# Low halves of column weights in two instructions, and the first attention unit's order tied to the last column, in a hybrid decoder step

## The chip, the core and the metric

The kernel runs on one core of a Trainium2 chip. Its engines are TensorE (PE, matrix products; PEld is its loading of weights), VectorE (DVE), ScalarE (ACT), GpSimd (POOL) and SyncE (SP, which here only issues DMAs). Each engine works through its own instructions in the order in which they were written out, and waits on semaphores for what the others make. The metric is the time of one execution on the device, in microseconds (us).

## The reference: what is computed

One step of a decoder layer for a prompt of 1024 rows of width 1024 and for 8 samples that each add one row. One input projection feeds three groups of heads; their outputs are gated, put side by side and projected back.

```python
h    = rms_norm(x, ln_g)
proj = h @ w_in                                   # 1024 x 3480
q, kv, gates, z_nsa, u, z_rw, q_mem, z_mem = split_in(proj)
# 8 heads: compressed blocks, selected blocks (top 16 of 64 rows), window of 512
o_nsa = gate_mix(sigmoid(gates), o_compressed, o_selected, o_window)
# 4 heads: S <- S diag(w) + (S(-kk)) (kk*a)^T + v k^T ;  y = S r, row after row
o_rw  = rwkv7_mix(u, ...)
# 4 heads: cross attention into 256 memory tokens
o_mem = softmax(q_mem @ k_mem.T) @ v_mem
cat   = concat(o_nsa * silu(z_nsa), o_rw * silu(z_rw), o_mem * silu(z_mem))
y     = x + cat @ w_out
```

With a prompt of 1024 rows there are 16 blocks of 64, so in the prompt all blocks that causality allows are selected. New key and value rows, the recurrent state and the memory's keys and values are outputs too.

## The kernel before

**Phase 1 projects.** `w_in` is taken in columns of 128. For each, `w_load` (L275) loads 512 KB into a raw buffer `wraw` (two buffers) from SP's queue, and `w_split` makes two float32r parts of it: ScalarE copies the high half `whi` (L283), VectorE subtracts to get the low half `wlo` (L284, 128 x 1024 in one instruction; one of the first columns gives it to GpSimd). `project` then goes through eight slices of the depth, k = 0 to 7, for each half of the prompt (512 rows): three matmuls a slice into `p_pr` (`h_k` high by `whi`, `h_k` low by `whi`, `h_k` high by `wlo`). PSUM holds three such buffers. A column of the gates z is finished by `do_z`: tanh on ScalarE (L318), one operation on VectorE (L319), stores to `z_d` (L321, L323). Row norms run on VectorE in many small instructions (L126 to L137), keys and queries are rotated at L384 to L400.

**What it is woven with.** The recurrent group works in four quarters (`rwkv_prep`, `rwkv_state`), with products `p_it`, `p_iy` on TensorE and copies `iT`, `iY`, `Ti` on the other engines between them (L920 to L967). `drive` takes its steps at a higher priority (AHEAD = 400), and the columns' steps fill in between. The keys, the compressed blocks and the memory's keys and values follow, with the last columns between them.

**The first unit.** An attention unit is a tile of 128 rows, a group of keys and a pair of heads, (i, g, hp); the units run from i = 7 down. For each head h of the pair and branch b (0 selected, 1 window), `attn_scores` makes scores `p_s` (keys split in `kh` and `kl`; two PSUM buffers of 1024), masks them and takes the row maximum on VectorE (L1502, called a mask from here on), then the exponential on ScalarE (L1508), a reciprocal (L1533), and a scaling on GpSimd (L1540). The transposes `p_pT` and their copies `pt` (VectorE L1464, ScalarE L1462) follow, then the products `p_o`. `first_scores` runs the scores of unit (7, 0, 0) between the steps of the last column, at the steps AT = (1, 5, 8, 11). The compressed branch goes through `p_sc` and `pcq` (L1419 to L1439).

**What sets the order.** Matmuls run in the order in which they are written (`InOrder` ties each to the one before it); on the other engines a scheduler chooses by priority, data and buffers, and `high_priority` moves what is inside it ahead. `in_turn` ties a step to the previous one of a chain kept in `self.mask`. In phase 2 the transposes have three PSUM banks (`pT`) and `p_o` has one (`pO`); the order of units is written out, with side work in four lanes (`step`, `slot`). Memory attention takes its maxima at L1596 on VectorE and its exponentials at L1598 on ScalarE.

## Time and profile before

| | us |
|---|---|
| median of 3 runs | 923.46 |
| runs | 923.26, 928.93, 923.46 |
| the profiled execution, whole | 927.17 |
| its span in the trace | 925.4 |
| TensorE busy in it | 888.4 |
| VectorE busy in it | 646.1 |
| ScalarE busy in it | 440.1 |

The trace is that of one execution, whose time lies above the median. A row of the timeline gives the start in us from the span's start, the duration, the engine, the line, the operation with output and inputs, and in brackets the engine's idle time before it with what ended that. The table of windows gives for each stretch its length and the busy time of TensorE, its weight loads, VectorE, ScalarE and GpSimd, then the granted TensorE clock, the DMA share and the GB/s. Where short instructions follow each other, a duration overlaps the next start a little; the difference of the starts is what an engine spends.

### The profile page before, as it was taken

What the parts mean: (1) busy time and instruction counts of PE and PEld (TensorE: products, weight loads), DVE (VectorE), ACT (ScalarE), POOL (GpSimd) and SP (SyncE); (2) the same over time, 40 slices, a digit from 0 to 9 for tenths busy, and PEclk for the clock granted to TensorE, in tenths of its full rate; (3) what the DMA queues carried; (4) which work ended last, traced back from release to release, by engine and by line L of the source; (5) the groups of instructions that cost most, each with busy time, mean ns of one, the idle gap of its engine ahead of it and who ended that gap; (6) DMA issues with size and microseconds to landing.
All of it is one profiled execution on the core that took longest, in us unless ns stands there. A gap on an engine that the chain in (4) does not pass through costs nothing.

```text
span 925.4 us, 24648 instructions
## 1 busy us (share of the span) xinstructions
PE 888.4 (96%) x9839; PEld 757.6 (82%) x9839; DVE 646.1 (70%) x2002; ACT 440.1 (48%) x1006; POOL 188.9 (20%) x280
## 2 busy tenths in 40 slices
PE   8999999999999999989998999999999998999998
PEld 8998888877878788758986788888878887887976
DVE  7768778964776459957567877676778986548454
ACT  7654324232443233324436676667666775324311
POOL 2000000000000000000105454444455665112010
PEclk9999999999999999999999999999999999999999
DMA  7431304141321303635638314422120037887561
GB/s 280 127 84 35 101 29 126 47 127 49 81 91 39 91 14 114 144 95 151 166 95 247 120 37 140 134 83 78 54 66 16 25 93 222 292 258 211 174 241 49
DMA packets 128298, 107.01 MB, mean 116 GB/s; under 512 B 26385, under 2 KB 113112, under 8 KB 128056
## 3 DMA queue, kind: packets, MB, share of 16 engines
q1 hardware_dynamic: 123096, 93.43, 34.7%
q0 software_dynamic: 3296, 10.75, 3.3%
q8 instruction: 78, 1.28, 0.6%
q10 hardware_dynamic: 1792, 1.26, 0.5%
q14 instruction: 36, 0.29, 0.1%
HBM read 84.72 MB, written 22.78 MB: 116 GB/s over the span
## 4 chain that ended last, share of the span: by engine, by line
PE 71%; DVE 17%; ACT 6%; issue 3%; DMA 1%; POOL 1%; SPq 0%; DVEq 0%; ACTq 0%; POOLq 0%
PE p_pr L87 26%; PE p_out L87 9%; PE p_s L87 5%; PE p_o L87 4%; PE p_pT L87 4%; PE p_hid L87 4%; ACT p L1508 3%; DVE p L1502 3%; PE p_pr L307 2%; PE p_tk L87 1%; DMA wraw<-in_w_in_dram 1%; DVE pt L1464 1%; PE p_it L87 1%; PE p_iy L87 1%; PE p_z L87 1%
## 5 line engine op out<-in xcount | busy, mean ns | idle before, releaser
L87 PE MATMUL p_pr<-h,whi 128*128 128x512 f32 (+2 forms) x1168 | 280.7, 334 | 2.0 <-DVE zt L319 2.0
L87 PEld LDWEIGHTS p_pr<-h,whi 128*128 128x128 f32 x1168 | 189.9, 189 | 21.0 <-issue 2.6
L87 PE MATMUL p_pr<-h,wlo 128*128 128x512 f32 (+2 forms) x584 | 188.1, 325 | 0.6 <-DVE wlo L284 0.6
L87 PEld LDWEIGHTS p_pr<-h,wlo 128*128 128x128 f32 x584 | 109.8, 189 | 10.4 <-DVE wlo L284 0.8
L1540 POOL TENSOR_SCALAR p<-p,fac,gates 128x640 f32<-128x640 f32 (+7 forms) x124 | 100.1, 819 | 77.4 <-DVE fac L1533 57.5
L1508 ACT ACTIVATE p<-p,nm 128x640 f32<-128x640 f32 (+7 forms) x124 | 89.2, 720 | 41.8 <-DVE nm L1502 38.0
L87 PE MATMUL p_pT<-ident,p 128*128 128x128 f32 x528 | 72.2, 279 | 8.4 <-DVE pt L1464 3.1
L1122 POOL MEMSET w2d<- 128x128 f32 x1 | 0.2, 208 | 375.7 <-DVE rq_r L137 375.7
L87 PEld LDWEIGHTS p_pT<-ident,p 128*128 128x128 f32 x528 | 56.6, 140 | 20.8 <-issue 6.0
L87 PE MATMUL p_o<-pt,vs 128*64 128x128 f32 x1056 | 68.4, 278 | 0.4 <-DVE cat L1578 0.4
L1502 DVE CUSTOM_DVE_ANT_0 p<-p_s,bmask 128x512 f32<-128x512 f32 (+7 forms) x96 | 60.6, 660 | 6.7 <-PE p_s L87 6.1
L87 PE MATMUL p_s<-kh,qs 128*128 128x512 f32 (+3 forms) x191 | 64.4, 350 | 0.8 <-DVE nm L1502 0.8
L283 ACT ACTIVATE whi<-wraw 128x1024 fp32r<-128x1024 f32 x34 | 36.0, 1059 | 60.0 <-PE p_pr L87 47.8
L87 PEld LDWEIGHTS p_o<-pt,vs 128*64 128x64 f32 x1056 | 57.3, 137 | 7.7 <-issue 3.8
L284 DVE TENSOR_TENSOR wlo<-wraw,whi 128x1024 fp32r<-128x1024 f32 x33 | 40.3, 1222 | 30.9 <-ACT whi L283 30.9
L87 PE MATMUL p_s<-kl,qs 128*128 128x512 f32 (+3 forms) x192 | 60.2, 334 | 0.0
L1464 DVE COPY pt<-p_pT 128x512 f32<-128x512 f32 (+1 forms) x72 | 48.1, 671 | 11.3 <-PE p_pT L87 11.1
L87 PE MATMUL p_out<-woh,chi 128*128 128x512 f32 x128 | 51.7, 404 | 0.0
L87 PE MATMUL p_out<-woh,clo 128*128 128x512 f32 x128 | 50.2, 392 | 0.4 <-DVE clo L2446 0.4
L87 PE MATMUL p_out<-wol,chi 128*128 128x512 f32 x128 | 49.9, 390 | 0.0
L1462 ACT ACTIVATE pt<-p_pT 128x512 f32<-128x512 f32 (+1 forms) x72 | 41.0, 576 | 13.5 <-PE p_pT L87 12.8
L87 PEld LDWEIGHTS p_s<-kh,qs 128*128 128x128 f32 x191 | 36.1, 189 | 3.5 <-DVE nm L1502 1.0
(554 smaller groups left out, 1789.7 us busy)
## 6 DMA issues: line engine op xcount, KB each, us to landing
wraw<-in_w_in_dram SPq DMA_DIRECT2D x34, 512.0 KB
pg<-in_c_pool_dram SPq DMA_DIRECT2D x32, 256.0 KB
pg<-in_c_pool_dram SPq DMA_DIRECT2D x48, 128.0 KB
x<-in_x_prompt_dram SPq DMA_DIRECT2D x8, 512.0 KB
z_d<-zt SPq DMA_DIRECT2D x16, 256.0 KB
cat<-z_d SPq DMA_DIRECT2D x8, 512.0 KB
xres<-in_x_prompt_dram POOLq DMA_DIRECT2D x16, 256.0 KB, 3.5
out_dram<-xres POOLq DMA_DIRECT2D x16, 256.0 KB, 3.4
```

What stands on the lines that cost most here:

```text
L87: self.last = getattr(self.engine, op)(*a, **k)
L283: nc.scalar.activation(hi[:, :, :n], raw[:, :, :n], AF.Copy)
L284: (low or nc.vector).tensor_tensor(lo[:, :, :n], raw[:, :, :n], hi[:, :, :n].bitcast(F32), op=OP.subtract)
L307: self.last_mm = self.pe.matmul(ps[:m, :b - a], w[:, k, :m], h[k][:, a:b], start=(k == 0 and i == 0), stop=(k == 7 and i == 2))
L1122: nc.gpsimd.memset(w2d[:], 0.0)
L1462: nc.scalar.activation(pt[:, :n], ps[:, :n], AF.Copy)
L1464: nc.vector.tensor_copy(pt[:, :n], ps[:, :n])
L1502: return V.tensor_tensor_reduce(halves(x), halves(ps), m, -1.0, 3.0e38, op0=OP.add, op1=OP.min, accum_out=nm[:, h, b:b + 1])
L1508: e = self.e_last = A.activation(x, x, AF.Exp, scale=-1.0, bias=nm[:, h, b:b + 1], accum_out=sm[:, h, b:b + 1])
L1540: self.g_last = nc.gpsimd.tensor_scalar(x, x, f[:, h, b:b + 1], gate[:, hd + h, 1 + b:2 + b], op0=OP.mult, op1=OP.mult)
```

## The change

It has five parts.

1. `w_split` makes the low half in two instructions, of the slices k 0 to 3 and 4 to 7, where VectorE makes it. The one on GpSimd stays whole.
2. `do_z`'s operation on VectorE is ordered behind the chain of `in_turn`, once there is one, and the last of them becomes the chain's end when the last column is done.
3. The chain of masks and reciprocals now holds for both units with (i, g) = (7, 0), (7, 0, 0) too. `first_scores` takes its steps at priority FIRST, and reciprocal and scaling are held back (`held`) and released by the second mask of the next branch.
4. In phase 2, the matmuls are tied to the last one of phase 1, the pool `pO` is made ahead of `pT`, so that the banks are dealt out otherwise, and the side work's steps around unit 1's scores stand in another order.
5. `attn_mem` takes its maxima at priority FIRST.

```diff
@@ w_split
-        (low or nc.vector).tensor_tensor(lo[:, :, :n], raw[:, :, :n], hi[:, :, :n].bitcast(F32), op=OP.subtract)
+        for k in ((slice(0, 8),) if low else (slice(0, 4), slice(4, 8))):
+            (low or nc.vector).tensor_tensor(lo[:, k, :n], raw[:, k, :n], hi[:, k, :n].bitcast(F32), op=OP.subtract)
@@ do_z
-            nc.vector.scalar_tensor_tensor(t[:, a:b], t[:, a:b], 1.0, ps[:, :b - a], op0=OP.add, op1=OP.mult)
+            with self.tc.issue_after(self.mask.ins) if self.mask else ExitStack():
+                self.last_zv = nc.vector.scalar_tensor_tensor(t[:, a:b], t[:, a:b], 1.0, ps[:, :b - a], op0=OP.add, op1=OP.mult)
@@ phase1
-        self.last_kd = None
+        self.last_kd = self.mask = None
@@ first_scores
-        self.held, self.mask = [], None
+        self.held = []
...
             if n in AT:
-                next(gen, None)
+                with self.tc.high_priority(offset=FIRST):
+                    next(gen, None)
+                    if n == AT[-1]:
+                        self.held.pop()()
...
-        self.lasts = [x.ins for x in (self.r_last, self.e_last, self.g_last)]
+        self.lasts = [x.ins for x in (self.mask, self.e_last, self.g_last)]
+        self.mask = self.last_zv
@@ attn_scores
-        begin = (i, g, hp) == (7, 0, 1)
+        begin = (i, g) == (7, 0)
...
-            while self.held and h == 0:
+            while self.held and (b, h) == (1, 0):
                 self.held.pop()()
...
-                if begin:
-                    self.in_turn(recip)
-                else:
-                    self.r_last = recip()
+                self.in_turn(recip) if begin else recip()
...
-            if begin and b == 0:
+            if begin and (hp, b) != (1, 1):
                 self.held.append(scale)
@@ attn_mem
-            V.tensor_reduce(nm[:], ps[:], axis=AX.X, op=OP.max, negate=True)
+            with self.tc.high_priority(offset=FIRST):
+                V.tensor_reduce(nm[:], ps[:], axis=AX.X, op=OP.max, negate=True)
@@ phase2
+            self.pO = P("pO", 1, space=PSUM, side="right")
             self.pT = P("pT", 3, space=PSUM, side="right")
-            self.pO = P("pO", 1, space=PSUM, side="right")
...
-            self.te = InOrder(tc, nc.tensor, None)
+            self.te = InOrder(tc, nc.tensor, last)
...
-            for k in range(2):
-                next(start)
-                step(0)
+            next(start)
+            step(0)
+            next(start)
...
             for _ in start:
                 pass
+            step(0)
```

In the rows that follow, each is one instruction (or `x n` of a kind) in the order in which its engine takes them; lines of the kernel after stand up to six higher than the same lines before.

TensorE at the last column, before, from the last passes of slice 3 on. `p_s` are scores, those of unit 0 with 128 and 512 columns (the last of its window branch), those of unit 1 with 512 and 512:

```order
L87 MATMUL p_pr<-h_3_813,wlo 128x512
L87 MATMUL p_s<-kh_6225,qs 128x128
L84 MATMUL p_s<-kh_6225,qs 128x512
L87 MATMUL p_s<-kl_6226,qs 128x512
L87 MATMUL p_s<-kh_6228,qs 128x512
L87 MATMUL p_s<-kl_6229,qs 128x512
L87 MATMUL p_s<-kl_6226,qs 128x128
L87 MATMUL p_s<-kh_6228,qs 128x512
L87 MATMUL p_s<-kl_6229,qs 128x512
L87 MATMUL p_pr<-h_4_897,whi 128x512
```

Four passes of unit 1 have slipped between the first pass of unit 0 and its other three.

The same place of TensorE after, where slice 3 ends:

```order
L87 MATMUL p_pr<-h_3_818,wlo 128x512
L87 MATMUL p_s<-kh_6254,qs 128x128
L87 MATMUL p_s<-kl_6255,qs 128x128
L87 MATMUL p_s<-kh_6257,qs 128x512
L87 MATMUL p_s<-kl_6258,qs 128x512
L87 MATMUL p_pr<-h_4_903,whi 128x512
```

Unit 0's four passes stand together, and unit 1's come after the column's last slice:

```order
L87 MATMUL p_pr<-h_7_919,whi 128x512
L87 MATMUL p_pr<-h_7_920,whi 128x512
L87 MATMUL p_pr<-h_7_919,wlo 128x512
L87 MATMUL p_s<-kh_6254,qs 128x512
L87 MATMUL p_s<-kl_6255,qs 128x512
L87 MATMUL p_s<-kh_6257,qs 128x512
L87 MATMUL p_s<-kl_6258,qs 128x512
L87 MATMUL p_sc<-cmask 128x4x64
```

So the four passes of unit 1 have moved behind four slices of the projection.

VectorE at the last column, before. `ISA` of 1024 or 640 is a mask, `ISA` of 1 reads its maximum, `RECIPROCAL` is of unit 0, `zt` is `do_z`'s operation:

```order
L1502 ISA p_6999,p_7001<-p_s,bmask 128x1024
L1502 ISA p_7001 128x1
L319 SCALAR_TENSOR_TENSOR zt<-zt,p_pr 128x256
L1502 ISA p_7000,p_7001<-p_s,bmask 128x1024
L1502 ISA p_7001 128x1
L1533 RECIPROCAL p_7001<-p_7001 128x2
L319 SCALAR_TENSOR_TENSOR zt<-zt,p_pr 128x264
L1502 ISA p_7001<-p_s,bmask 128x640
L1502 ISA p_7001 128x1
L1502 ISA p_7002,p_7001<-p_s,bmask 128x640
L1502 ISA p_7001 128x1
L1533 RECIPROCAL p_7001<-p_7001 128x2
```

A `zt` stands between the first two masks, and the reciprocal of the selected branch is ahead of the window branch's masks.

VectorE there after:

```order
L1508 ISA p_7032,p_7034<-p_s,bmask 128x1024
L1508 ISA p_7034 128x1
L1508 ISA p_7033,p_7034<-p_s,bmask 128x1024
L1508 ISA p_7034 128x1
L321 SCALAR_TENSOR_TENSOR zt<-zt,p_pr 128x256
L321 SCALAR_TENSOR_TENSOR zt<-zt,p_pr 128x264
L1508 ISA p_7034<-p_s,bmask 128x640
L1508 ISA p_7034 128x1
L1539 RECIPROCAL p_7034<-p_7034 128x2
L1508 ISA p_7035,p_7034<-p_s,bmask 128x640
L1508 ISA p_7034 128x1
L1539 RECIPROCAL p_7034<-p_7034 128x2
```

The two masks of the selected branch stand together, both small `zt` behind them, and the reciprocal one mask later.

VectorE in the recurrent group's work, at 391 us of the trace, before. `nr_y` and `rq_a` are of a row norm, `iT` of the recurrent state:

```order
L127 TENSOR_SCALAR rq_g<-rq_a 128x1
L284 TENSOR_TENSOR wlo<-wraw,whi 128x1024
L384 TENSOR_TENSOR nr_y<-p_tk,rq_r 128x512
L128 TENSOR_SCALAR rq_a<-rq_a 128x1
L385 TENSOR_TENSOR nr_y<-nr_y,gains 128x512
L948 STREAM_TRANSPOSE iT<-p_it 128x256
```

The low half is one instruction ahead of the norm.

There, after:

```order
L127 TENSOR_SCALAR rq_g<-rq_a 128x1
L285 TENSOR_TENSOR wlo<-wraw,whi 128x512
L386 TENSOR_TENSOR nr_y<-p_tk,rq_r 128x512
L128 TENSOR_SCALAR rq_a<-rq_a 128x1
L285 TENSOR_TENSOR wlo<-wraw,whi 128x512
L387 TENSOR_TENSOR nr_y<-nr_y,gains 128x512
L954 STREAM_TRANSPOSE iT<-p_it 128x256
```

Its second part has moved behind two instructions of the norm. In the same way, the second part stands behind `iY`, `Ti` and `zt` at 318 us (where the whole one stood ahead of them), and behind three `zt` at 266 us.

More of the change, by code (lines that the diff above doesn't have):

```diff
@@ L1693, in phase2 @@
             self.load_z(7)
+            last = self.te.last
             self.te = nc.tensor
             self.attn_setup(P)
-            self.te = InOrder(tc, nc.tensor, None)
+            self.te = InOrder(tc, nc.tensor, last)
             units = [(i, g, hp) for i in range(7, -1, -1) for g in range(2) for hp in range(2)]
```

## The prediction

> **What bounds the kernel now.** I read the page first, then the windows of the stages that the change touches, then TensorE's waits, and the timeline at the longest of them.
>
> ```profile
> span 925.4 us, 24648 instructions
> PE 888.4 (96%) x9839; PEld 757.6 (82%) x9839; DVE 646.1 (70%) x2002; ACT 440.1 (48%) x1006; POOL 188.9 (20%) x280
> ...
> 240.00:280.00 40.00, 37.97 (x220) 32.36 (x219) 28.95 (x98) 15.70 (x28) 0.00 (x0) 0.96 0.30 88
> 480.00:520.00 40.00, 35.10 (x272) 29.13 (x271) 30.58 (x80) 22.09 (x49) 17.32 (x20) 1.00 0.79 232
> ```
>
> TensorE works 888.4 of 925.4 us, so all that a reordering can win is what lies in 37.0 us of gaps. The change leaves the number of matmuls as it is, and VectorE has 279.3 us idle (925.4 − 646.1): extra work there costs only where TensorE waits for it. The stage 480 to 520, where the first attention unit starts beside the last column, has 4.9 us of the gaps (40 − 35.10); the others that the change touches are single waits, shown below.
>
> **Part 1, the first unit.** Its rows on TensorE, each with the wait before it in brackets:
>
> ```profile
> 488.64 0.50 PE L84 MATMUL p_s<-kh,qs 128*128 128x512 f32 x1 [1.13 <-DVE p L1502]
> 495.75 0.38 PE L87 MATMUL p_sc<-cmask 128*128 128x256 f32 x1 [1.11 <-DVE zt L319]
> 497.46 0.66 PE L87 MATMUL p_pT<-ident,p 128*128 128x128 f32 x4 [0.47 <-DVE pcq L1422]
> 498.93 0.66 PE L87 MATMUL p_pT<-ident,p 128*128 128x128 f32 x4 [0.82 <-DVE pcq L1422]
> 500.36 0.66 PE L87 MATMUL p_pT<-ident,p 128*128 128x128 f32 x4 [0.77 <-ACT pt L1462]
> 509.77 0.66 PE L87 MATMUL p_pT<-ident,p 128*128 128x128 f32 x4 [0.60 <-DVE pt L1464]
> ```
>
> They sum to 4.90 us, which is the stage's whole gap. The first arises because unit 1's scores stand among the last four passes of unit 0's and wait for a score buffer that a mask holds. With the new order these four passes run together, the four slices `h_4` to `h_7` follow, and unit 1's scores come after them: the 1.13 us go. VectorE shows what then decides:
>
> ```profile
> 481.46 1.21 DVE L1502 CUSTOM_DVE_ANT_0 p<-p_s,bmask 128x1024 f32<-128x1024 f32 x1
> ...
> 484.26 0.42 DVE L319 SCALAR_TENSOR_TENSOR zt<-zt,p_pr 128x256 f32<-128x256 f32 x1 [1.58 <-ACT zt L318]
> 484.60 1.22 DVE L1502 CUSTOM_DVE_ANT_0 p<-p_s,bmask 128x1024 f32<-128x1024 f32 x1
> ...
> 490.46 0.82 DVE L1502 CUSTOM_DVE_ANT_1 p<-p_s,bmask 128x640 f32<-128x640 f32 x1 [1.88 <-PE p_s L87]
> ...
> 495.03 0.67 DVE L319 SCALAR_TENSOR_TENSOR zt<-zt,p_pr 128x512 f32<-128x512 f32 x1
> ```
> ```profile
> 492.76 0.40 PE L87 MATMUL p_pr<-h,wlo 128*128 128x512 f32 x1
> ...
> 505.74 1.97 PE L87 MATMUL p_o<-pt,vs 128*64 128x128 f32 x32
> ```
> ```profile
> 493.20 0.60 ACT L318 ACTIVATE zt<-p_pr 128x512 f32<-128x512 f32 x1 [0.66 <-PE p_pr L87]
> ...
> 495.13 1.15 ACT L1508 ACTIVATE p<-p,nm 128x1024 f32<-128x1024 f32 x1 [0.72 <-DVE nm L1502]
> ```
>
> Before, unit 0's second mask sits behind a `zt` that waits 1.58 us for ScalarE; with both masks in turn it starts at 482.7, when the first ends, instead of 484.60. The last mask of unit 0 waits for its scores: these come 1.13 plus about 1.0 us sooner (the stall, and unit 1's four score passes ahead of it at some 0.25 each, an estimate from the 0.50 of the first one shown, of which half overlaps). So it starts near 488.3 instead of 490.46 and ends at 489.1. The last `p_pr` ends near 491.0 (492.76 + 0.40 − 2.1). The large `zt` follows after its tanh (0.60) and its own 0.67, near 492.2 against 495.7, so `p_sc` no longer waits 1.11 for it.
>
> From there the chain is not TensorE's any more: a mask of 1.21, an exponential of 1.15, and both engines' copies between the transposes, while VectorE leaves few gaps. Laid out with these durations in the new order, the third group of transposes starts at 494.25 behind the `pcq` add (new wait 0.3), the fourth at 496.1 behind ScalarE, whose copy follows unit 1's first exponential (1.4), and the seventh at 501.4 behind a `pt` copy (1.65): 3.35 of new waits in place of 4.90, and `p_o` near 504.7 instead of 505.74. **−1.5 us.** Bounds: −4.9 if no new wait arises, and 0 if VectorE's chain, 30.58 of 40 us busy over the stage, only shifts the waits. I take the laid-out value, nearer to 0.
>
> The `pcq` multiply of the compressed branch goes behind the two masks of unit 2, 2.4 us:
>
> ```profile
> 505.18 1.58 DVE L1439 TENSOR_TENSOR pcq<-pcq,c_r 128x512 f32<-128x512 f32 x1
> ```
> ```profile
> 512.61 0.60 PE L87 MATMUL p_pT<-ident,pcq 128*128 128x128 f32 x4
> ```
>
> Its reader on TensorE starts 5.9 us after it ends, so I cost that at nothing; without that cover it would be 2.4 us, two masks. The swap of the two PSUM pools moves only addresses; the first `p_o` starts some 10 us after the large `zt` has read the bank that it takes over: nothing. GpSimd's scaling of unit 0 moves behind one mask, and loads on SP's queue behind stores of `z` and `q`; the scaled rows are read by the transposes, which wait later for other things in the layout above: nothing.
>
> **Part 2, low halves in two.** 33 instructions become 66. Rows for a 1024 and a 512:
>
> ```profile
> 389.69 1.21 DVE L284 TENSOR_TENSOR wlo<-wraw,whi 128x1024 fp32r<-128x1024 f32 x1
> 390.82 0.68 DVE L384 TENSOR_TENSOR nr_y<-p_tk,rq_r 128x512 f32<-128x512 f32 x1
> 391.42 0.14 DVE L128 TENSOR_SCALAR rq_a<-rq_a 128x1 f32<-128x1 f32 x1
> ```
>
> By starts, 1024 take 1.13 us and 512 take 0.60: a split costs 2 × 0.60 − 1.13 = 0.07 us, 2.3 us of VectorE in all, in 279 us of idle time. Whether that ever lies on the path is rival (b). [...]
>
> Where the first half's reader can go on, or something urgent stands between the halves in the new order:
>
> ```profile
> 30.44 0.39 PE L87 MATMUL p_pr<-h,wlo 128*128 128x256 f32 x1 [0.64 <-DVE wlo L284]
> ...
> 273.18 0.73 PE L87 MATMUL p_pr<-h,whi 128*128 128x512 f32 x2 [2.03 <-DVE zt L319]
> ...
> 318.02 1.23 DVE L284 TENSOR_TENSOR wlo<-wraw,whi 128x1024 fp32r<-128x1024 f32 x1 [1.14 <-ACT whi L283]
> 319.28 0.43 DVE L960 COPY iY<-p_iy 32x256 f32<-32x256 f32 x1
> 319.63 0.42 DVE L944 COPY Ti<-p_it 32x256 f32<-32x256 f32 x1
> 320.11 0.69 PE L87 MATMUL p_it<-Ti,iY 32*32 32x32 f32 x30 [1.29 <-DVE Ti L944]
> PE p_h L223 <- DVE h L242: 0.8, 2, 0.5
> ```
>
> At 30 us TensorE waits for the low half itself; the first half is there 0.5 sooner, of which I count −0.4 (0 to −0.64). At 273 the second half moves behind the `zt` that TensorE waits for: one half, −0.6 (0 to −0.7). At 320 both copies come one half sooner, −0.6 (0 to −1.29). In the last row, near 64 us, the `h` of the second half of the prompt come in another order with the halves, two waits of 0.4: −0.2 (0 to −0.8). Together −1.8.
>
> The other side: a raw buffer is loaded again only when the second half has read it.
>
> ```profile
> 267.60 0.38 SPq L275 DMA_DIRECT2D wraw<-in_w_in_dram  x1
> ...
> 390.96 0.38 SPq L275 DMA_DIRECT2D wraw<-in_w_in_dram  x1
> ...
> 280.80 1.06 ACT L283 ACTIVATE whi<-wraw 128x1024 fp32r<-128x1024 f32 x1 [9.22 <-PE p_pr L87]
> ...
> 395.35 1.06 ACT L283 ACTIVATE whi<-wraw 128x1024 fp32r<-128x1024 f32 x1 [2.85 <-DMA wraw<-in_w_in_dram]
> ...
> 400.03 0.75 PE L87 MATMUL p_it<-iT,iY 32*32 32x32 f32 x64 [0.72 <-DVE iY L920]
> ```
>
> At 391 a `nr_y` (0.60) and an `rq_a` slip between the halves, so the load starts about 0.75 later (0.68 and the split's 0.07), and so do `whi`, which has been waiting for it, the low halves, and the `iT` and `iY` queued behind them, for which TensorE already waits: **+0.7** (0 to +1.5, if the copies have to queue behind both halves twice). At 266 the second half moves behind the three `zt`, so that load starts near 274.5 instead of 267.60. At the 4.4 us that the other took from issue to its reader (390.96 to 395.35) it lands near 279; ScalarE wants it at 280.80 and had until then waited for TensorE. That is 1.9 us of cover, so 0.
>
> **Part 3, maxima of the memory scores.** They move up by one to a few places; the place with a price:
>
> ```profile
> 745.75 0.49 ACT L1508 ACTIVATE p<-p,nm 128x256 f32<-128x256 f32 x1
> 746.25 0.57 ACT L1462 ACTIVATE pt<-p_pT 128x512 f32<-128x512 f32 x1
> ...
> 746.87 0.39 PE L87 MATMUL p_sm<-mkh,qs 128*128 128x256 f32 x1 [1.39 <-ACT pt L1462]
> 751.60 1.06 PE L87 MATMUL p_pT<-ident,p 128*128 128x128 f32 x8 [0.34 <-ACT pt L1462]
> ```
>
> With the maximum earlier, the scheduler puts the two memory exponentials ahead of the four of the attention, where ScalarE had a gap, and its copy `pt` behind three of these (0.49 each) instead of four: −0.5 at 746.87. At 751.60 the copy also stands one exponential sooner, but its transposes are hardly sooner: −0.1. **−0.6** (−1.7 if both waits vanish; +0.6, the length of a 512-wide row of VectorE by starts, if a maximum now holds up a mask).
>
> Sum: −1.5 − 1.8 + 0.7 − 0.6 = **−3.2**. The profiled execution took 927.17 us (span 925.4 and 1.8 around it), 3.7 above the median of the three runs, 923.46; the granted clock of 0.96 in 240 to 280 shows that it had slowed matmuls there, which the others need not have. Taken from its own time the sum gives 924.0; what I set against the runs is the median less the same sum, 920.3, rounded to 920.5.
>
> **The rivals.**
> (a) The first unit's chain closes fully: −4.9 instead of −1.5, so 923.46 − 6.6 = 916.9. For it: the masks come up to 3 us sooner. Against: VectorE and ScalarE have to copy every group of transposes between masks and exponentials, and 3.05 of my 3.35 us of new waits are behind such copies.
>
> (b) The gains are given back: the 2.3 us of VectorE come on the path, because it is nearly full just where the halves stand. Then the halves' −1.8 turn into +0.5, and 923.46 − 1.5 + 0.5 + 0.7 − 0.6 gives 922.6; if the first unit wins nothing either, 924.1. For it: the stage 0 to 520 holds all halves, and its gaps behind VectorE are many and short. Against: TensorE has 96% of the time and runs behind VectorE at few places. [...]
>
> (c) Slower: the late load at 274.5. It is issued after three `zt`, and must land within 6.3 us (280.80 − 274.5). Past that, TensorE stands until `whi` and the low half are made, 1 us for 1. The sign turns 3.2 us beyond, at a landing of 9.5 us against 4.4; at 11 us the time would be 920.3 + 4.7 = 925.0. For it: `z` is stored on the same queue at that time, ahead of the load. Against: the load near 391 stands among stores too, and took 4.4.
>
> (d) The change doesn't do what it says: the order shows on every engine that it does, so this has no chance of its own.
>
> **How the numbers follow.** My forecast (−2 to −5) has 0.50, (b) 0.28, (a) 0.10, (c) 0.12. The likeliest gives 920.5 us, and its own range is 918.5 to 921.5. For 8 in 10 the range takes in (b) with both its values and (a) near its middle, and reaches the upper bound of the load near 391 (+0.8) and the small end of (c): 916.5 to 925.0. About 1%, 9.2 us, is what a measurement of this kernel can tell from no change. The waits at the touched places sum to 12.1 us (4.90, 0.64, 2.03, 1.29, 0.8, 0.72, 1.39, 0.34), of which a gain of 9.2 would need three quarters; a loss of 9.2 needs a landing of 19 us in (c): faster 0.03, same 0.94, slower 0.03.
>
> **What would show it.** Right: no wait for a score buffer among unit 0's last passes, the first `p_o` near 504.7 where it began at 505.74 (less what earlier stages gain); the waits at 30, 273 and 320 shorter by about half a `wlo`; the wait near 400 longer; `p_sm`'s near 747 shorter. Wrong: waits in 480 to 520 summing to 4.9 again or more, a `whi` near 281 waiting for its load, or VectorE's busy time up by far more than 2.3 us (by starts), or a new long wait on TensorE anywhere else.

## The result, and the profile after

Runs of the two kernels in turn on one chip, nine of each: 924.74 us before (923.0 to 928.93), **918.95 us** after (916.66 to 920.69), a ratio of 0.9926 with a 95% interval of 0.9911 to 0.9942. The kernel is 6 to 7 us faster: 5.8 by the medians, 6.8 by the ratio. The profiled execution of the changed kernel took 918.86 us, that of before 927.17, so this pair differs by 8.3, more than the medians do. Why is part of what follows.

The head of the page after, and the two stages that were shown of before (columns as there: length, busy time of PE, PEld, DVE, ACT, POOL, granted clock, DMA share, GB/s):

```profile
span 917.1 us, 24696 instructions
PE 883.7 (96%) x9839; PEld 754.5 (82%) x9839; DVE 648.8 (71%) x2035; ACT 439.4 (48%) x1006; POOL 187.7 (20%) x280
...
240.00:280.00 40.00, 38.50 (x238) 33.30 (x237) 30.86 (x97) 17.04 (x33) 0.00 (x0) 1.00 0.31 89
480.00:520.00 40.00, 35.62 (x292) 29.70 (x291) 32.86 (x87) 24.91 (x57) 20.24 (x23) 1.00 0.72 217
```

Two things changed, not one. TensorE's gaps went from 37.0 to 33.4 us (span less PE), and its busy time from 888.4 to 883.7 for the same 9839 matmuls. A reordering explains the first, not the second; the clock in the first stage, 0.96 before and 1.00 now, points to the rest. VectorE has 2.7 us more work; 2.3 by starts were foreseen.

TensorE's timeline of the changed kernel, the rows at the touched places (start, duration, what ran, and in brackets the wait just before):

```profile
271.72 0.73 PE L87 MATMUL p_pr<-h,whi 128*128 128x512 f32 x2 [1.50 <-DVE zt L321]
...
316.29 0.69 PE L87 MATMUL p_it<-Ti,iY 32*32 32x32 f32 x30 [0.74 <-DVE Ti L950]
...
491.53 0.66 PE L87 MATMUL p_pT<-ident,p 128*128 128x128 f32 x4 [1.44 <-DVE pcq L1428]
493.29 0.66 PE L87 MATMUL p_pT<-ident,p 128*128 128x128 f32 x4 [1.11 <-ACT pt L1468]
498.12 0.44 PE L87 MATMUL p_pT<-ident,p 128*128 128x128 f32 x2 [0.90 <-ACT qs L1398]
500.34 1.97 PE L87 MATMUL p_o<-pt,vs 128*64 128x128 f32 x32
504.10 0.66 PE L87 MATMUL p_pT<-ident,p 128*128 128x128 f32 x4 [0.33 <-DVE pt L1470]
...
739.44 0.36 PE L87 MATMUL p_sm<-mkh,qs 128*128 128x256 f32 x1
...
757.04 1.09 PE L87 MATMUL p_o<-pt,vs 128*64 128x128 f32 x16 [1.16 <-DVE cat L1581]
```

The wait of 0.64 at 30 us is gone, those of 2.03 and 1.29 behind `zt` and `Ti` are 1.50 and 0.74, the 1.13 for a score buffer and the 1.11 for `zt` are gone with others in their place, and `p_sm`, which waited 1.39, waits no more. New is the 1.16 for `cat` in the last row.

To see where the 8.3 us of the profiled pair came from, I took the start of the same matmul in both traces at the borders of each stretch; a stretch that is shorter by itself has gained there. "Waits" is the change of TensorE's waits in it, as far as they are over 0.15 us each, "busy" the rest (shorter gaps with it).

| stretch of before, us | change | waits | busy | what lies there |
|---|---|---|---|---|
| 3.3 to 9.3 | −0.40 | +0.21 | −0.61 | the start, before any change |
| 9.3 to 31.0 | −0.35 | −0.45 | +0.10 | low half at 30, less a longer wait at 17 |
| 31.0 to 99.8 | −0.22 | −0.27 | +0.05 | `h` near 64 |
| 269.9 to 279.9 | −2.13 | −0.53 | −1.60 | `zt` at 273 |
| 279.9 to 330.0 | −0.83 | −0.77 | −0.06 | `Ti` at 320, and one of 0.22 at 308 |
| 371.7 to 483.8 | −0.20 | +0.01 | −0.21 | the load near 391 |
| 483.8 to 519.7 | −1.66 | −1.12 | −0.54 | the first unit |
| 739.0 to 753.0 | −2.07 | −1.73 | −0.34 | memory scores |
| 753.0 to 767.6 | +0.66 | +0.43 | +0.23 | the new wait for `cat` |
| 767.6 to 782.9 | −1.58 | −0.22 | −1.36 | no moved work |

The stretches left out sum to +0.4.

Two rows stand out: −1.60 and −1.36 of busy time, where the matmuls are the same. Windows of 1 us in the trace of before show what that is (the sixth figure after the length is the granted clock):

```profile
272.00:273.00 1.00, 0.00 (x0) 0.00 (x0) 1.00 (x5) 0.00 (x0) 0.00 (x0) 1.00 0.00 0
273.00:274.00 1.00, 0.82 (x4) 0.70 (x5) 1.00 (x5) 0.00 (x0) 0.00 (x0) 1.00 0.55 171
274.00:275.00 1.00, 1.00 (x4) 0.80 (x3) 0.20 (x1) 0.00 (x0) 0.00 (x0) 0.55 0.94 347
275.00:276.00 1.00, 1.00 (x4) 0.72 (x4) 0.00 (x0) 0.00 (x0) 0.00 (x0) 0.50 0.78 273
276.00:277.00 1.00, 1.00 (x4) 0.81 (x3) 0.00 (x0) 0.00 (x0) 0.00 (x0) 0.50 0.00 0
277.00:278.00 1.00, 1.00 (x5) 0.83 (x4) 0.00 (x0) 0.00 (x0) 0.00 (x0) 0.74 0.00 0
278.00:279.00 1.00, 1.00 (x9) 0.83 (x8) 0.06 (x1) 0.00 (x0) 0.00 (x0) 1.00 0.00 0
```

The window of 272 is all wait (the 2.03 for `zt`). Just behind it TensorE runs at half clock, 4 matmuls in a microsecond instead of 9. The missing clock of the four windows is 0.45 + 0.50 + 0.50 + 0.26 = 1.71 us, which at half clock is a stretch of 3.4 us. A second such stretch stands at 779 to 783 and a third at 321 to 326, each with 1.71 us missing too. In the trace after one is left, at 317 to 321 (0.41 + 0.50 + 0.50 + 0.29 = 1.70). So the pair differs by two of them, the 3.0 us of these two rows. They are the larger part of the 4.7 us that TensorE's busy time lost (888.4 to 883.7); the rest lies in small pieces, 0.61 at the start among them, and has no cause shown.

I call this a half-clock stretch. All that I looked at were 1.71 us of missing clock or a multiple of it, so each run's mean granted clock counts them: (1 − clock) × span / 1.71. Before's profiled run has 0.994, that is 3; after's has 0.998, one. (The clock is given to 0.001, half a stretch.)

### The profile page after: what moved, and what is told of

Its sections match the earlier page's. It is cut to its first block, busy times and chain, and to the rows that moved or that the text cites. A ratio compares the mean times of both kernels' runs of the same rounds, so it can differ in the third digit from the quotient of the medians.

```text
span 917.1 us, 24696 instructions
## 1 busy us (share of the span) xinstructions
PE 883.7 (96%) x9839; PEld 754.5 (82%) x9839; DVE 648.8 (71%) x2035; ACT 439.4 (48%) x1006; POOL 187.7 (20%) x280
## 5 line engine op out<-in xcount | busy, mean ns | idle before, releaser
L285 DVE TENSOR_TENSOR wlo<-wraw,whi 128x512 fp32r<-128x512 f32 x66 | 44.3, 685 | 27.8 <-ACT whi L283 27.8
```

Source lines behind the costliest of these rows:

```text
L285: (low or nc.vector).tensor_tensor(lo[:, k, :n], raw[:, k, :n], hi[:, k, :n].bitcast(F32), op=OP.subtract)
```

## The experiments

Twelve more kernels were measured. The stretches made plain times of the parts hard to compare, so the table gives, beside each kernel's runs, their mean count, and the mean time with 1.2 us taken off for each stretch. The 1.2 is a fit: over the 94 runs of the changed kernel and of all variants but the one with 5 long waits, each taken against its own kernel's mean, a run is 0.69 ± 0.05 us longer for each microsecond of missing clock, and over the 58 runs of before that were taken beside them, 0.72 ± 0.11. 0.7 × 1.71 is 1.2. That is less than the 1.71 which TensorE loses; later waits that get shorter would account for it, but I didn't show that. The uncertainty of such a mean is some 0.5 us, of a difference of two some 0.6.

| kernel | median us (runs) | ratio to before | stretches a run | mean less 1.2 each |
|---|---|---|---|---|
| before | 925.35 (58) | 1 | 2.8 | 922.0 |
| after | 918.95 (9) | 0.9926 [0.9911, 0.9942] | 1.7 | 916.8 |
| e1 halves alone | 922.11 (5) | 0.9959 [0.9946, 0.9972] | 2.2 | 919.4 |
| e3 maxima alone | 924.67 (11) | 0.9996 [0.9984, 1.0008] | 3.5 | 920.8 |
| e5 first unit alone | 923.18 (12) | 0.9975 [0.9962, 0.9988] | 2.3 | 920.3 |
| e2 after without halves | 921.44 (6) | 0.9952 [0.9936, 0.9968] | 2.5 | 918.2 |
| e4 after without maxima | 919.44 (5) | 0.9931 [0.9918, 0.9944] | 0.8 | 918.4 |
| e6 low halves in four | 918.43 (7) | 0.9946 [0.9923, 0.9968] | 2.6 | 917.0 |
| e12 one column whole | 918.71 (5) | 0.9920 [0.9908, 0.9933] | 1.6 | 916.9 |
| e9 `cat` product raised too | 919.66 (5) | 0.9941 [0.9929, 0.9954] | 1.8 | 917.9 |
| e10 `zt` raised too | 923.04 (12) | 0.9976 [0.9962, 0.9990] | 4.4 | 917.6 |
| e8 five short waits | 925.37 (12) | 1.0001 [0.9988, 1.0014] | 1.3 | 923.5 |
| e7 five long waits | 950.74 (5) | 1.0279 [1.0259, 1.0299] | 8.4 | 940.7 |
| e11 the long waits filled | 944.76 (5) | 1.0196 [1.0183, 1.0209] | 1.8 | 942.4 |

### The parts, one by one and one left out

**e1_halves**: before, with the loop over two slices in `w_split` and nothing else.

```diff
-        (low or nc.vector).tensor_tensor(lo[:, :, :n], raw[:, :, :n], hi[:, :, :n].bitcast(F32), op=OP.subtract)
+        for k in ((slice(0, 8),) if low else (slice(0, 4), slice(4, 8))):
+            (low or nc.vector).tensor_tensor(lo[:, k, :n], raw[:, k, :n], hi[:, k, :n].bitcast(F32), op=OP.subtract)
```

> The kernel before with the low halves in two instructions, nothing else. Theory (the parts add up, each at its own place): the traces of before and after differ by about 2.0 us at the places of the halves (0.35 at 30 us, 0.2 near 64, 0.5 at 273, 0.2 near 290, 0.6 at 320, 0.2 to 0.4 near 400), so this kernel is 2.0 us faster than before, ratio 0.9978. Rival A (VectorE's extra time comes on the path, as the prediction's second rival has it): 0 to 0.5 us slower. Rival B (the prediction's sum with the late load at 391 us costing 0.7): 1.1 us faster, and TensorE's wait for iY near 400 us grows to 1.4 us.

Measured: 0.9959, 3.2 us by the means, of which 2.5 without the stretches; 2.0 were expected. TensorE's waits are shorter at the same places and by much the same amounts as in the changed kernel: −0.36 (9 to 31 us), −0.27 (31 to 100), −0.52 (270 to 280), −0.22 (the one at 308) and −0.55 (319 to 330). The wait for `iY` near 400, which rival B has grow to 1.4, is not there at all.

**e2_no_halves**: the changed kernel with the loop taken back out.

```diff
-        for k in ((slice(0, 8),) if low else (slice(0, 4), slice(4, 8))):
-            (low or nc.vector).tensor_tensor(lo[:, k, :n], raw[:, k, :n], hi[:, k, :n].bitcast(F32), op=OP.subtract)
+        (low or nc.vector).tensor_tensor(lo[:, :, :n], raw[:, :, :n], hi[:, :, :n].bitcast(F32), op=OP.subtract)
```

> The kernel after with whole low halves. Theory: the first unit and the maxima alone remain, 1.6 and 1.5 us: 3.1 us faster than before, ratio 0.9966, and about 2 us slower than after. Rival A (the halves cost VectorE time): as fast as after or faster, 5.8 us or more under before. Rival B: 4.7 us under before.

Measured: 0.9952, so the halves are worth 2.4 us here by the means and 1.4 without the stretches. Both ways they win: the cost on VectorE doesn't eat the gain.

**e3_max**: before, with the maxima at the higher priority alone.

```diff
-            V.tensor_reduce(nm[:], ps[:], axis=AX.X, op=OP.max, negate=True)
+            with self.tc.high_priority(offset=FIRST):
+                V.tensor_reduce(nm[:], ps[:], axis=AX.X, op=OP.max, negate=True)
```

> The kernel before with the maxima of the memory scores at attention's priority, nothing else. Theory (the second product of memory scores no longer waits for ScalarE's copy at all, since it gets the bank of the first product, whose exponentials are now done before): the wait of 1.39 us near 747 us is gone, the next one of 0.34 too, 0.4 us come back as a wait for the output sum near 763: 1.5 us faster, ratio 0.9984. Rival (the prediction's: the copy comes one exponential sooner, and no more): a wait of 0.9 us is left near 747 us, 0.6 us faster, ratio 0.9994.

Measured: 0.9996 and no measurable gain, though the trace shows what it should: 739 to 753 is 2.07 us shorter, both waits there gone. TensorE's timeline of e3 has the same new wait as the changed kernel:

```profile
762.52 1.80 PE L87 MATMUL p_o<-pt,vs 128*64 128x128 f32 x16 [1.16 <-DVE cat L1578]
```

That takes a part of the gain back (0.66 of the 2.07 in the changed kernel's table above), and its runs have 3.5 stretches where those of before have 2.8. Without them the part is worth 1.2; by the plain means it is 0.4, which the runs cannot tell from nothing.

**e4_no_max**: the changed kernel with the priority taken back out.

```diff
-            with self.tc.high_priority(offset=FIRST):
-                V.tensor_reduce(nm[:], ps[:], axis=AX.X, op=OP.max, negate=True)
+            V.tensor_reduce(nm[:], ps[:], axis=AX.X, op=OP.max, negate=True)
```

> The kernel after with the maxima of the memory scores at their old priority. Theory: halves and first unit remain, 2.0 and 1.6 us: 3.6 us under before, ratio 0.9961, the wait near 747 us back at 1.4 us. Rival (0.6 us is all that the maxima bring, and the rest of the gain lies elsewhere): 5.2 us under before.

Measured: 0.9931, as fast as the changed kernel within the uncertainty, which the expectation of 0.9961 missed. The wait of 1.39 at `p_sm` is back (at 740.26), but the runs have 0.8 stretches instead of 1.7. Without them this kernel is 1.6 slower and 3.6 under before, which is what the theory has; the plain time is nearer to its rival (5.2 under before). So what the maxima bring rests on the traces and on the count of stretches, not on plain times.

**e5_unit**: the changed kernel with both of these taken back, so that the parts of the first unit stand alone.

> The kernel after with whole low halves and with the maxima at their old priority: the parts around the first unit alone. Theory: TensorE's waits in 484 to 520 us shrink by 1.6 us and nothing else changes, so about 1.6 us under before, plus 1.7 us for each stretch of half TensorE clock that goes with those waits (the records show these stretches, 3.4 us each, behind waits; two of them near 495 us in the kernels without this part, one or none in those with it): 2 to 4 us under before, mean granted clock higher. Rival (the order of the first unit brings no more than its waits): 1.6 us, clock as before.

Measured: 0.9975, or 2.3 us by the means and 1.7 without the stretches, of which it has 2.3 a run instead of 2.8. That lies between theory and rival and does not decide. The two stretches near 495 us that the theory speaks of are not in the trace of before: its clock from 480 to 520 is 1.00, as it is in the changed kernel. The three parts alone give 2.5 + 1.2 + 1.7 = 5.4; the whole gives 922.0 − 916.8 = 5.2. They add up, and the means of the runs differ by a further 1.3, which is 1.1 stretches fewer.

### What makes a half-clock stretch

The theory was that TensorE's own waits bring them about. Five waits were put into the projections of phase 1, where TensorE otherwise has next to none (1.1 us from 60 to 180 us in the changed kernel), by a product that needs a copy which VectorE makes late. The added product writes rows that the next real product starts afresh, so the output doesn't use it; its time comes on top.

**e7_gaps_long**: seven copies each, close to 4 us of wait.

```diff
+        self.calls = getattr(self, "calls", 0) + 1
+        if self.calls in (9, 11, 13, 15, 17):
+            with self.tc.high_priority(offset=AHEAD):
+                ps, x = pss[0], self.ev.tile([128, 520], F32, name="gap", tag="ev", bufs=2)
+                self.pe.matmul(ps[:, :128], self.ident[:], self.ident[:], start=True, stop=True)
+                for c in range(4):
+                    self.nc.vector.tensor_copy(x[:, 128 * c:128 * c + 128], ps[:, :128])
+                for _ in range(3):
+                    self.nc.vector.tensor_copy(x[:, :512], x[:, :512])
+                self.pe.matmul(ps[:, :128], x[:, :128], self.ident[:], start=True, stop=True)
```

> The kernel after, which in five places between about 60 and 130 us, where TensorE has next to no gaps, waits for a copy of its own result through VectorE, some 3 us each. Theory (a wait of TensorE costs its own length and, with some chance that grows with it, a stretch of 3.4 us at half clock, worth 1.7): time over after is the five waits plus 1.7 us for each added stretch; granted clock falls from 0.997 to about 0.99, with stretches of half clock right behind most of the five waits. Rival (the stretches have nothing to do with waits): only the five waits are added, clock as after, no stretch in 60 to 130 us.

**e8_gaps_short**: the same with one copy each.

```diff
-                for c in range(4):
+                for c in range(1):
                     self.nc.vector.tensor_copy(x[:, 128 * c:128 * c + 128], ps[:, :128])
-                for _ in range(3):
+                for _ in range(0):
```

> The same with one short copy in each of the five places, a wait of 0.5 to 1 us each. Theory: five times the wait, and at most one or two stretches of half clock more than after. Rival (every wait of any length brings one): clock down by 0.009, as with the long ones.

**e11_filled**: e7 with 14 products of the identity in front of the last one of each group, and three of the four narrow copies made from the first one; the products are overwritten.

```diff
+                for _ in range(14):
+                    self.pe.matmul(ps[:, :128], self.ident[:], self.ident[:], start=True, stop=True)
                 self.pe.matmul(ps[:, :128], x[:, :128], self.ident[:], start=True, stop=True)
```

> The kernel with five long waits (as in e7_gaps_long, 3.8 us each), in which TensorE now does 14 products of the identity while it waits for VectorE's copies; their results are overwritten. Theory (half clock follows idleness of TensorE, not the place or the chain): the added time is the five waits still, about 19 to 21 us over after, but the stretches of half clock behind them are gone: 1 to 2 in an execution as in after, instead of 8.4; so some 10 us under e7_gaps_long. Rival (something else at these places brings the half clock, VectorE's copies or the length of the chain): 7 or more stretches and the time of e7_gaps_long.

The waits that TensorE had at these products (total us, times, longest), then the window of 60 to 180 us, first of e7:

```profile
PE p_pr L87 <- DVE gap L313: 19.1, 5, 4.4
...
60.00:180.00 120.00, 99.80 (x1338) 83.59 (x1337) 85.48 (x281) 37.57 (x87) 0.00 (x0) 0.91 0.17 48
```

of e8:

```profile
PE p_pr L87 <- DVE gap L311: 3.8, 4, 1.2
...
60.00:180.00 120.00, 115.04 (x1509) 99.63 (x1509) 94.32 (x311) 48.26 (x108) 0.00 (x0) 1.00 0.24 68
```

and of e11:

```profile
PE p_pr L87 <- DVE gap L310: 3.8, 4, 1.2
...
PE p_pr L87 <- DVE gap L314: 1.3, 2, 1.1
...
60.00:180.00 120.00, 113.50 (x1526) 98.76 (x1525) 89.13 (x292) 41.42 (x95) 0.00 (x0) 1.00 0.18 51
```

With 3.8 us of wait each on average the clock falls to 0.91 in this stage of e7; the other two have 1.00. The first of the five shows how it follows, in e7's TensorE timeline and windows:

```profile
74.77 0.49 PE L87 MATMUL p_pr<-ident,gap 128*128 128x128 f32 x2 [4.07 <-DVE gap L313]
...
75.00:76.00 1.00, 1.00 (x5) 0.85 (x5) 0.11 (x1) 0.00 (x0) 0.00 (x0) 0.72 0.00 0
76.00:77.00 1.00, 1.00 (x4) 0.66 (x2) 0.00 (x0) 0.00 (x0) 0.00 (x0) 0.50 0.00 0
```

All five waits (3.0 to 4.4 us) have a stretch right behind them, one a double, which is the some 0.09 × 120 = 10.8 us of missing clock in this stage, about six stretches; e7's five runs show 7 to 10 each. The four that e8's profile shows, 1.0 each on average, have none, and its runs no more than the changed kernel's. In e11 VectorE does a chain as long as in e7, but TensorE has other products to run and waits 5.1 us in six pieces, by the rows above: no stretch in the stage, and 1.8 a run in all. So at these places the clock falls where TensorE stands idle for 3 us and more, not where a product is late. e11's time missed its expectation: it is 6 us under e7 rather than 10, because the 28 instructions that fill each wait last 3.39 us by its timeline, and with the 5.1 us of waits left (3.8 and 1.3 in the rows above) that is more than e7's 19.1. It stands 26 us over the changed kernel, e7 32. e8's 6.4 us are its 3.8 of waits and what the added products take.

A wait of 3 us is not needed for a stretch: in the trace of before a wait of 2.03 at 273, with TensorE busy throughout the 3 us ahead of it (1.00 in each window from 268 to 271), was followed by one, and the one in the changed kernel's trace, at 317, stands behind a wait of 0.74, while e8's four waits (1.0 on average, 1.2 at most) have none. Nor does the same wait always bring one: e2, e3 and e5 still have the wait of 2.03 or 2.02 at that place, and no stretch behind it. The window of e2 around it:

```profile
268.00:284.00 16.00, 13.97 (x95) 12.71 (x93) 10.60 (x35) 5.01 (x11) 0.00 (x0) 1.00 0.35 104
```

One in four profiles, then, for the same wait: a chance, not a rule. What decides it, no run shows.

### Two more priorities, and the halves taken further

**e10_z**: the changed kernel, with `zt` of phase 1 raised as well, to take the 1.50 at 271.72 away.

```diff
-            nc.scalar.activation(t[:, a:b], ps[:, :b - a], AF.Tanh, scale=0.5)
-            with self.tc.issue_after(self.mask.ins) if self.mask else ExitStack():
+            with self.tc.high_priority(offset=0 if self.mask else AHEAD):
+              nc.scalar.activation(t[:, a:b], ps[:, :b - a], AF.Tanh, scale=0.5)
+              with self.tc.issue_after(self.mask.ins) if self.mask else ExitStack():
```

> The kernel after with the gates' two operations at the priority of the recurrent work until the first unit begins. VectorE's zt, for which TensorE still waits 1.5 us at 272 us, goes 22 instructions ahead. Theory: that wait vanishes and with it the stretch of half clock behind it in those executions that have one: 1.5 to 2.5 us under after. Rival (the instructions that now stand behind zt are late instead, and a wait for one of them takes its place): same time as after.

Measured: 923.04, 4 us slower than the changed kernel. The wait at 272 is gone, but others are longer. TensorE's timeline of e10, and the window behind its waits:

```profile
315.21 0.88 PE L87 MATMUL p_it<-Ti,iY 32*32 32x32 f32 x30 [1.14 <-DVE Ti L951]
...
393.53 0.31 PE L87 MATMUL p_iy<-iT,AM 32*32 32x32 f32 x12 [1.25 <-issue]
398.37 0.69 PE L87 MATMUL p_iy<-iT,AM 32*32 32x32 f32 x32 [0.95 <-DVE iT L949]
...
400.00:411.00 11.00, 10.78 (x110) 8.73 (x106) 2.32 (x8) 2.17 (x7) 0.00 (x0) 0.54 0.38 106
```

Behind these waits TensorE is at half clock for 10 us, three stretches in a row. The runs have 4.4 instead of 1.7, which at 1.2 each is 3.3 of the 4 us; the waits from 268 to 440 us cancel in the trace (−1.50 at 272, +0.59 near 315, +0.90 from 367 on). Its runs are also the plainest view of the price: 925.07 us at a mean clock of 0.987, 920.34 at 0.996.

**e6_quarters**: the low halves in four instructions each.

```diff
-        for k in ((slice(0, 8),) if low else (slice(0, 4), slice(4, 8))):
+        for k in ((slice(0, 8),) if low else (slice(0, 2), slice(2, 4), slice(4, 6), slice(6, 8))):
```

> The kernel after with the low halves in four instructions instead of two, 66 more on VectorE. By starts a 512 takes 0.60 us and a 256 takes 0.33, so 66 x 0.03 to 0.07 = 2 to 4.6 us more of VectorE. Theory (this time is hidden, and the first quarters help only where TensorE waits for a low half): within 1 us of after. Rival (the prediction's second: VectorE's fixed cost lies on the path): 2 to 4 us over after.

Measured: 918.43, the same by the median and without the stretches (917.0 against 916.8), although VectorE has 652.6 us of work instead of 648.8. By the plain mean it is 1.3 slower, with 2.6 stretches a run instead of 1.7. The wait near 272 is gone altogether, that at 316 is 0.48.

**e12_391**: the changed kernel with the low half of the one column near 391 us whole again.

```diff
-        for k in ((slice(0, 8),) if low else (slice(0, 4), slice(4, 8))):
+        self.split = getattr(self, "split", 0) + 1
+        for k in ((slice(0, 8),) if low or self.split == 31 else (slice(0, 4), slice(4, 8))):
```

> The kernel after, with the one low half near 387 us (391 in before) whole, so that its buffer is loaded again 0.75 us sooner. The prediction's term: whi, the low halves, iT and iY come 0.7 us sooner and TensorE's waits near 394 us with them, 0.7 us under after. Theory after the traces (the later load landed in 3.6 us instead of 4.4, so the reader was not late): load issued 0.7 sooner, whi less than 0.3 us sooner, time as after.

Measured: 918.71, the same. How long the load takes there differs from kernel to kernel. SP's issue and ScalarE's reader, in the changed kernel and then in e12:

```profile
388.07 0.39 SPq L275 DMA_DIRECT2D wraw<-in_w_in_dram  x1
...
391.67 1.06 ACT L283 ACTIVATE whi<-wraw 128x1024 fp32r<-128x1024 f32 x1 [1.77 <-DMA wraw<-in_w_in_dram]
```
```profile
385.84 0.39 SPq L275 DMA_DIRECT2D wraw<-in_w_in_dram  x1
...
390.85 1.06 ACT L283 ACTIVATE whi<-wraw 128x1024 fp32r<-128x1024 f32 x1 [3.59 <-DMA wraw<-in_w_in_dram]
```

From issue to reader: 3.6 us and 5.0 us, and 4.4 before the change. Measured from the same matmul near 368 us, e12's load is issued 1.0 us sooner than the changed kernel's, and its reader starts 0.4 later. The other traces mostly go the same way: the five with this low half whole (before, e2, e3, e5, e12) have 4.0 to 5.0, the eight with it in two (after, e1, e4, e7, e8, e9, e10, e11) 3.3 to 3.9, but for the 4.8 of e10. So a load issued later mostly took less time; why, no run shows.

**e9_cat**: the changed kernel with the product into `cat` raised, to take the new wait of 1.16 away.

```diff
-            self.nc.vector.tensor_tensor(cat, cat, po[:], op=OP.mult)
+            with self.tc.high_priority(offset=2 * FIRST):
+                self.nc.vector.tensor_tensor(cat, cat, po[:], op=OP.mult)
```

> The kernel after with the product of gates and p_o on VectorE (L1581) at twice the attention's priority. It is what TensorE waits 1.16 us for at 757 us, a wait that came with the maxima's priority. Theory: that wait shrinks by about 1 us, and the executions have fewer stretches of half clock behind it (1 instead of 1.7): 1 to 2 us under after. Rival (the row norms and masks that it passes are late instead): same time as after, a wait for nm or pcq near 757 us.

Measured: 919.66, no gain, as the rival has it. The wait at 757 is gone, and e9's timeline shows what came instead, 3.03 us in three places:

```profile
693.96 0.66 PE L87 MATMUL p_pT<-ident,p 128*128 128x128 f32 x4 [1.04 <-DVE pt L1470]
695.73 0.60 PE L87 MATMUL p_sv<-ident,rw_b 128*8 128x128 f32 x4 [1.11 <-ACT pt L1468]
...
760.57 0.33 PE L87 MATMUL p_s<-kh,qs 128*128 128x128 f32 x1 [0.88 <-DVE nm L1508]
```

## Why the prediction was right, and where its sum was not

The side (a small gain, within 1%) and the range held, and the time lies 1.6 us under the point. That it lies so near is partly luck: the point was taken from the median of three runs, 923.46, and the nine of before have 924.74, so the change is −5.8 by the medians, beyond the −2 to −5 that the forecast gave itself. The sum was −3.2; with the stretches taken off the runs show −5.2 for the reordering, and −1.3 beside it that was in no term.

**The first unit, −1.5: right in size, in part by luck.** −1.66 in the trace, 1.7 in e5. No wait for a score buffer is left among unit 0's passes, and the first `p_o` starts at 500.34; what precedes 483.84 had gained 4.11, so by the clock of before that is 504.45, against the 504.7 of the layout. The first two waits come where it put them, the third is for `qs` and not for a `pt` copy, and the shares are others: 3.78 in sum (1.44, 1.11, 0.90, 0.33) against 3.35, the first much longer than the 0.3 foreseen. VectorE's and GpSimd's rows of the changed kernel show why (`s_in` are small rows for the 8 samples):

```profile
484.07 0.82 DVE L1508 CUSTOM_DVE_ANT_1 p<-p_s,bmask 128x640 f32<-128x640 f32 x1 [1.16 <-PE p_s L87]
...
486.64 0.76 DVE L1823 TENSOR_TENSOR s_in<-gains,rope 8x96 f32<-8x96 f32 x1
...
487.67 0.76 DVE L1824 TENSOR_TENSOR s_in<-gains,rope 8x96 f32<-8x96 f32 x1
488.36 1.04 DVE L1827 TENSOR_SCALAR s_in<-s_in 8x192 f32<-8x192 f32 x1
489.33 0.66 DVE L321 SCALAR_TENSOR_TENSOR zt<-zt,p_pr 128x512 f32<-128x512 f32 x1
```
```profile
486.16 1.14 POOL L1543 TENSOR_SCALAR p<-p,gates 128x640 f32<-128x640 f32 x1 [0.58 <-DVE p L1539]
487.29 1.05 POOL L1543 TENSOR_SCALAR p<-p,p,gates 128x640 f32<-128x640 f32 x1
```

Unit 0's last mask starts at 484.07, which is 488.2 by the old clock (488.3 foreseen). The large `zt` ends at 490.0, or 494.1 by the old clock, and not near 492.2: the chain between those two was laid out 1.9 us too short. The tanh is done at 487.41, as laid out, but nine `s_in` rows stand ahead of `zt`, from 485.98 on. Six of them take 0.24 or less; the two of 0.76 each end 0.10 us after a GpSimd scaling, and the one of 1.04, beside which GpSimd only fills tiles, took 0.24 in the trace of before. These three make up 1.8 of the 1.9 us; the last section comes back to them. That the sum still held is partly luck: the waits alone fell by 1.1, and TensorE's own part of the stage got 0.54 shorter, which had no term. **Rival (a)** would have needed 4.9.

**The halves, −1.8: right place by place.** At 30 us −0.45 (−0.4 foreseen; the whole 0.64 is gone, but a wait at 17 us is 0.19 longer), at 273 −0.53 (−0.6), at 320 −0.55 (−0.6), near 64 −0.27 (−0.2): −1.8. A wait of 0.22 at 308 is gone too; it is gone in e2 and e5 as well, whose halves are whole, so it is not counted here.

**Their other side: the late load at 266, costed at nothing: right.** It was issued behind the three `zt` (273.70, or 274.6 by the old clock; 274.5 foreseen), and ScalarE still waited for TensorE and not for it. SP's and ScalarE's rows of the changed kernel:

```profile
273.70 0.39 SPq L275 DMA_DIRECT2D wraw<-in_w_in_dram  x1
...
277.75 1.06 ACT L283 ACTIVATE whi<-wraw 128x1024 fp32r<-128x1024 f32 x1 [7.10 <-PE p_pr L87]
```

So **rival (c)** did not happen; the load was there 4.05 us after its issue at the latest.

**The load near 391, +0.7: the step that was wrong.** The stretch of 371.7 to 483.8 became 0.20 shorter, not longer, the wait near 400 (0.72 before) is 0.28, and e12, which takes the split out there, takes the same time within the uncertainty. The start of the load was argued well enough, its landing was not: the term took 4.4 us from issue to reader as fixed, and the kernels with the split have 3.3 to 3.9 with one exception, those without 4.0 to 5.0. A delay of 0.75 of the issue is lost in that. One trace could not have shown the term either way: the kernels without the split differ among themselves in this stretch by 1.3 us (from 0.59 shorter than before in e2 to 0.73 longer in e3).

**Rival (b), VectorE's added work comes on the path: wrong.** 2.7 us more busy time here cost nothing that e1 and e2 could show, nor did e6's further 3.8.

**The maxima, −0.6: the order right, the relief of `p_sm` not as argued.** Both waits vanished, 1.73 us, which was the bound. The reasoning had ScalarE's copy `pt` one exponential sooner, 0.5. ScalarE's rows of the changed kernel show the copy where it was expected, behind three exponentials and after the memory's:

```profile
737.22 0.46 ACT L1602 ACTIVATE pmem<-p_sm,nm_m 128x256 f32<-128x256 f32 x1
...
739.47 0.50 ACT L1514 ACTIVATE p<-p,nm 128x256 f32<-128x256 f32 x1
739.96 0.57 ACT L1468 ACTIVATE pt<-p_pT 128x512 f32<-128x512 f32 x1
```

But `p_sm` runs at 739.44, before this copy has begun: it doesn't wait for it any more. By the kernel's text it comes from the same pool of banks as `p_pT`; that with the memory exponentials done early it takes another bank, free sooner, is inferred, since the trace names no banks. So this wait for a buffer did not shrink by the time that its holder moved; it vanished. Against the 2.07 stand 0.66 with the new wait for `cat`: −1.4 in all from the trace, 1.2 and 1.6 from e3 and e4 without the stretches, but only 0.4 and 0.6 by their plain means. Over the four terms, sizes off by −0.2, 0, −0.9 and −0.8 make up nearly all of the 2.0 between −3.2 and −5.2.

**The clock: the thing that was left out.** The prediction saw the 0.96 in the stage of 240 to 280 and put it down to this one execution, "which the others need not have". It is half right: a stretch does not fall in the same place each time, since the same wait had one in only one of four profiles. But this run had 3 stretches, and the 58 runs of before had 1 to 4 each, 2.8 on average. Their number is part of the kernel's time. The changed kernel has 1.7 a run, which is the 1.3 us beyond the sum. That idle time of TensorE brings stretches is shown for the waits of 3.0 to 4.4 us that were put in (e7, e11). That the fall from 2.8 to 1.7 comes from the fewer waits is argued, not shown: TensorE's gaps in the profiled runs don't go with the count. They are 37.0 us in before (2.8 stretches a run), 33.4 in the changed kernel (1.7), 33.6 in e4 (0.8), 34.0 in e3 (3.5) and 31.1 in e10 (4.4).

**Open:** which waits the stretches follow in runs without a profile, and why single runs of one kernel differ so much (e6 has 1 to 5, e10 2 to 7). The 0.40 at the start, ahead of any change, is taken for noise.

## What to carry to other kernels

Read the mean granted clock of every run before comparing times: here it counts half-clock stretches of TensorE, and a difference of one or two of them, 1.2 us each by the fit, is as large as a small edit, so parts are compared with that taken off. A long wait of TensorE can cost more than its length: the five of 3 us and more that were put in each had a slow stretch behind them, shorter ones sometimes (the 2.03 at 273 in one profile of four). A local priority moved a wait here each time that it removed one (the maxima to `cat`, `cat` to `nm` and `pt`, `zt` to `Ti` and `iT`), so look at who is queued behind, on that engine, before raising anything.

## What the runs showed of the hardware that I had not expected

Besides the clock, with its stretches of 3.4 us, small VectorE rows that take up to 1.04 us and end with a GpSimd instruction beside them. The new wait for `cat` stems from a VectorE instruction of 8x4 elements. VectorE's and GpSimd's rows of the changed kernel:

```profile
755.24 1.04 DVE L137 SCALAR_TENSOR_TENSOR rq_r<-rq_t,rq_r 8x4 f32<-8x4 f32 x1
756.31 0.41 DVE L2405 TENSOR_TENSOR rw_a<-rw_a,rq_r 8x256 f32<-8x256 f32 x1
...
756.73 0.25 DVE L1581 TENSOR_TENSOR cat<-cat,p_o 128x128 f32<-128x128 f32 x1
```
```profile
755.23 1.04 POOL L1435 TENSOR_TENSOR pcq<-pcq,c_m 128x512 f32<-128x512 f32 x1 [0.74 <-DVE rq_t L136]
```

This form takes 0.15 at its two other places in the trace and here 1.04: it starts 0.01 us after GpSimd's product of two inputs and ends with it, and `cat`, three instructions on, is late by that 0.9. All nine profiled kernels with the maxima raised but not `cat` (the changed one, e2, e3, e6, e7, e8, e10, e11 and e12) show this same row of 1.04; before, e1, e4, e5 and e9 don't. It is no single case. Eight VectorE instructions of the trace before and eleven of this one take over 0.2 us longer than the median of their line and form beside a GpSimd instruction that is not a fill (`MEMSET`), and all end 0.01 to 0.10 us after one; the two `s_in` of 0.76 above are among them. No run took it apart. If the GpSimd product beside it is what lengthens the row of 1.04, some 0.9 of the new wait of 1.16 us hang on it. Not every row beside GpSimd is longer: before, the same instruction took 0.17 at 760.98, although a GpSimd scaling had run since 760.88 and went on to 761.33. So which work of GpSimd goes with longer rows of VectorE, and why, stays open.
